# Order bounds, a delayed step, spaced fetches and another DMA queue in a fused DeltaNet / GLA / forgetting-attention layer

## The chip, the cores and the metric

The kernel runs on one core of one Trainium2 chip. The metric is the device time of one execution in microseconds (us). What a measurement of this kernel can tell from no change is about 0.5%, some 5 us.

A core has several engines that run at the same time and wait for each other on semaphores: TensorE (PE in the profile, with its weight loads as PEld), VectorE (DVE), ScalarE (ACT), GpSimd (POOL), and the sync engine (SP), which here only issues DMA transfers. ScalarE and GpSimd can issue DMA transfers too, from the same instruction queue that holds their computations. Each engine works through its own queue in order, so an instruction that waits also holds everything queued behind it on that engine.

## The reference

One layer of a hybrid decoder: RMSNorm, one input projection (2048 to 7585 columns), three token mixers on disjoint groups of heads, a SiLU gate on each, one output projection, the residual, and a final RMSNorm. 16 meta tokens stand in front of 512 tokens. Everything is float32.

```python
h = rms_norm(x, norm_w)                                  # 528 tokens x 2048
(dq, dk, dv, dz, db, da, gq, gk, gv, gz, gl, fq, fk, fv, fz, ff) = split_cols(h @ w_in)
# A) gated DeltaNet, 6 heads x 128, in chunks; state S per head
v_new = u_c - w_c @ s
o     = qd @ s + qk_c @ v_new
s     = s * gl + kd.T @ v_new
o_dn  = gated_head_norm(o, dz, dn_norm_w)                # times silu(dz)
# B) GLA, 5 heads (dk 64, dv 128), decay per key dimension
attn  = einsum('bhid,bhjd,bhijd->bhij', q_c, k_c, exp(g_i - g_j))
o     = (q_c * exp(g)) @ s + attn @ v_c
# C) softmax attention with a forget-gate bias, 5 heads x 128
o_fox = softmax(q @ k.T + c_t - c_s) @ v * silu(fz)
out   = rms_norm(x + concat(o_dn, o_gla, o_fox) @ w_out, final_norm_w)
```

## The kernel before

**Products.** Every float32 weight half (128 x 1024) is loaded by SP into one of two `raw` buffers and split into two parts: `hi` by a cast on ScalarE (`split`, L165, named `whi` or `whio` in the profile) and `lo` by a subtraction on VectorE (L166, `wlo`, `wloo`). The normalised input has two parts too, `xh` and `xl`. A product is then three matmuls: hi by xh, hi by xl, lo by xh (`inproj_part`, L233). A block of 128 columns has 16 slices of the contraction; with meta tokens it has two accumulation chains of 264 columns and so 96 matmuls, without them one chain of 512 columns and 48 matmuls. Each matmul of the input projection is noted in the list `order`; `head` has the place at which a block begins.

**Order.** The instructions of each engine are put in order by a scheduler that plays the program through with its own clock. The kernel steers it in three ways. `later` (L1278) puts a small matmul behind the matmul of a given place in `order` (a lower bound). `sooner` (L1275) puts the matmul of a given place behind the small matmul (an upper bound). `paced` (L171) puts an instruction behind the latest weight split. These bounds only order the queues; they are no semaphores between engines. Blocks come in this order: two `dz` and the `dk`, `dv`, `dq` of the second DeltaNet group, the `gz`, then gk 0, gq 0, gv 0, gv 1, gk 1, gq 1, gv 2, gv 3, gk 2, gv 4, fk 0, fv 0, fq 0, fz 0, fk 1, fq 1, and then the heads of the forgetting attention in pairs of blocks. `gq` and `fq` have one chain, `gk` and `gv` two.

**Mixing.** `dn_mix` (L789) runs the DeltaNet recurrence of a group of three heads over four blocks of 128 tokens: `pks` (L847, keys by state), `zz` on VectorE (L851), `py` (L855), its copy `y` on ScalarE, `psn` (L862), the new state `sn` on VectorE, and, off the recurrence, `po` (L874) and the gate `pt` (L811, L814). For the second group, `soon` (L817) gives `pks`, `py` and `psn` of block b the upper bounds MIX + 56 b + 0, 20 and 38, counted from the first matmul of gv 1; MIX is 10. The triangular inverse before it (`dn_inverse`, L681) has lower bounds of its own: `pm` at PM, `pn` (L753) of the first group at PM + 72.

**GLA.** `gla_pair(p)` (L909) has seven levels per pair of heads (block sizes 64 to 1). For each level VectorE takes two differences (L971, L973), ScalarE an exponential (L974; L977 at the last level), VectorE two products into the shared `kq` buffers (L975, L979), and TensorE many small matmuls `pss` (L993). `PLACE` (L192) gives lower bounds to these groups, and to others, by tile name. Then come the states (`pg0`, `pgn`, `gst`) and the outputs `pgo` (L1057, L1063). The third pair has one head.

**The last step of x.** The later heads of the forgetting attention use products of sums of input blocks. For those, `x_last` (L508) overwrites the second token half of `xh` and `xl` of eight slices: for each slice a load `xe` by GpSimd's queue into a buffer called `row` (seven of these in all), a scaling on ScalarE (L514), L515 on VectorE, a cast (L517) and L518. The first use is the sixth product of the first pair of blocks (`inproj_pair`, L522).

**Tail.** The gated heads' outputs go through DRAM. `fetch` (L1095) loads six of them back during the products of the last pair; `split_o` (L1303) splits them into `oh` and `ol`, all paced. `run` (L1361) is the output projection of these heads, `begin` (L1325) loads a 128 x 512 piece of the residual tokens into `accs` through ScalarE's queue, `add` (L1347) adds a finished bank to it on VectorE. `first_sums` (L591) forms sums of other heads on GpSimd (L596, L597) once their loads `zr` have landed.

Of the kernel before, what the change touches and what calls it, by code (L numbers as in the profile page):

```python
# [82 lines left out]
def tile_hybrid_trunk(ctx, tc, xT, xtok, mtok, w_gate, w_in, w_out, w_dn, consts, lmask, fin_w, out, dbg=None):  # L83
# [104 lines left out]
    def part(name, n=512):  # L188
# [3 lines left out]
    PLACE = {  # L192
        "pss00": (('gv', 3), 50),
        "pss01": (('gv', 3), 56),
        "pss02": (('gv', 3), 72),
        "pss03": (('gv', 3), 82),
        "pss04": (('gv', 3), 92),
        "pss05": (('gk', 2), 6),
        "pss06": (('gk', 2), 16),
        "pg00": (('gk', 2), 44),  # L200
        "pss10": (('fk', 0), 84),
# [7 lines left out]
        "pss23": (('fk', 1), 60),  # L209
        "pss25": (('fk', 1), 84),  # L210
    }
# [296 lines left out]
    def x_last():  # L508

        for k in range(NK):  # L510
            r = row(f"xe{k}")[:, :T]
            nc.gpsimd.dma_start(out=r.rearrange("p (i t) -> p i t", i=2), in_=xT[:, k : k + 9 : 8, HT:])
            x12, x22 = r[:, :HT], r[:, HT:]
            A.activation(x12, x12, AF.Copy, scale=nwc[:, k : k + 1])  # L514
            V.scalar_tensor_tensor(out=x22, in0=x22, scalar=nwc[:, k + 8 : k + 9], in1=x12, op0=ALU.mult,  # L515
                                   op1=ALU.subtract)
            A.copy(xh[k][:, HT:], x22)  # L517
            V.tensor_tensor(out=xl[k][:, HT:], in0=x22, in1=xh[k][:, HT:].bitcast(F32), op=ALU.subtract)  # L518
# [162 lines left out]
    def dn_inverse(g, st):  # L681
# [61 lines left out]
        for q in range(2):  # L743
# [8 lines left out]
            for n in ns:  # L752
                mm = PE.matmul(pn[:, n - q * 6, :], an[64:128, n, 0:64], uf[64:128, n, 64:128],  # L753
                               start=True, stop=True)
                if g + n == 0:
                    behind(mm, PM[g] + 72)
            m2 = t15(f"m2{g}{q}", (64, 6, 64))
# [31 lines left out]
    def dn_mix(g, st):  # L789
# [27 lines left out]
        def soon(mm, b, i):  # L817
            if g == 1:
                sooner.append((mm.ins, MIX + 56 * b + (0, 20, 38)[i]))

# [22 lines left out]
        for b in range(NB):  # L843
# [10 lines left out]
            for j in range(H):  # L854
                mm = PE.matmul(py[:, j * P : (j + 1) * P], uf[:, b * H + j, :], z[:, j, :], start=True, stop=True)  # L855
            soon(mm, b, 1)
            y = t15(f"y{g}{b}")
            A.copy(y, py[:, : H * P].rearrange("p (h d) -> p h d", h=H))
            if b < NB - 1:
                pn = psm.tile([P, 512], F32, tag="m", name=f"psn{g}{b}")  # L860
                for j in range(H):
                    mm = PE.matmul(pn[:, j * P : (j + 1) * P], kd[:, b * H + j, :], y[:, j, :], start=True, stop=True)  # L862
                soon(mm, b, 2)
                sn = t15(f"sn{g}{b}")
# [41 lines left out]

    kts, qts, ats = [], [], []

    def gla_pair(p):  # L909
# [52 lines left out]
        def scores(s, li):  # L962
# [13 lines left out]
            else:  # L976
                A.activation(dv[:, :, 1, :], dv[:, :, 1, :], AF.Exp, scale=SC)  # L977
                kx = kT[:, NM:]
            V.tensor_tensor(out=qxv[:, :, 1, :], in0=qv[:, :, 1, :], in1=dv[:, :, 1, :], op=ALU.mult)  # L979
            return kx, qx  # L980
# [73 lines left out]
        for e in range(ne):  # L1054
            for b in range(NB):
                bs = slice(b * P, (b + 1) * P)
                PE.matmul(po[e][:, bs], at[:, e * NB + b, :], vt[:, e, bs], start=b == 0, stop=False,  # L1057
                          skip_group_check=True)
        for b in range(NB):
# [35 lines left out]
    def fetch(i):  # L1095
        if i < 6:
            if i % 3 == 0:
                zrow.append(six.tile([P, 3, S], F32, tag="six", name=f"zp{i}"))
            nc.sync.dma_start(out=zrow[-1][:, i % 3], in_=zd[SH + i])

# [202 lines left out]
    def split_o(i):  # L1303
# [6 lines left out]
        hi, lo = part(f"oh{i}"), part(f"ol{i}")  # L1310
        paced(A.copy(hi, z), sub(lo, z, hi.bitcast(F32)))
        oparts[i] = hi, lo
# [12 lines left out]
    def begin(tb, cc, load=True):  # L1325
# [4 lines left out]
        if load:  # L1330
            nc.scalar.dma_start(out=acc[tb, cc], in_=xtok[tb * P : (tb + 1) * P, cc * 512 : (cc + 1) * 512])

# [225 lines left out]
```

## Time and profile before

| | |
|---|---|
| three runs | 1014.11, 1014.30, 1019.31 us; median 1014.3 |
| the profiled execution | 1014.57 us, of which the span from first to last instruction is 1012.9 |
| mean granted TensorE clock | 0.992 |
| chain of work that ended last | PE 87%, DMA 4%, DVE 3%, issue 2%, ACT 2% |
| DMA moved | 186.05 MB, mean 184 GB/s |

How to read it. Busy time of an engine is the union of its instructions. A row of waits says who waited for whom: total us, times, longest. A row of the timeline has its start, its length in us, engine, line, operation, tiles (output, arrow, inputs), shapes and, in brackets, how long the engine was idle before it and what ended that. Rows of stretches give from:to, length, busy time of PE, PEld, DVE, ACT and POOL with the number of instructions, then the granted TensorE clock (1.00 is full), the busy share of the DMA engines and GB/s. ACTq and SPq mark an engine's queue as it issues transfers.

### The profile page before, as it was taken

What the parts mean: (1) busy time and instruction counts of PE and PEld (TensorE: products, weight loads), DVE (VectorE), ACT (ScalarE), POOL (GpSimd) and SP (SyncE); (2) the same over time, 40 slices, a digit from 0 to 9 for tenths busy, and PEclk for the clock granted to TensorE, in tenths of its full rate; (3) what the DMA queues carried; (4) which work ended last, traced back from release to release, by engine and by line L of the source; (5) the groups of instructions that cost most, each with busy time, mean ns of one, the idle gap of its engine ahead of it and who ended that gap; (6) DMA issues with size and microseconds to landing.
All of it is one profiled execution on the core that took longest, in us unless ns stands there. A gap on an engine that the chain in (4) does not pass through costs nothing.

```text
span 1012.9 us, 19786 instructions
## 1 busy us (share of the span) xinstructions
PE 987.0 (97%) x7782; PEld 901.0 (89%) x7782; DVE 661.3 (65%) x1427; ACT 478.0 (47%) x1045; POOL 239.3 (24%) x272
## 2 busy tenths in 40 slices
PE   8999999999999999998999999899999999999996
PEld 7899999899999888898999988799999988788885
DVE  6356877966658984334766748576775665868573
ACT  6754534334455334244545444646554452644254
POOL 1032423413324334211213222211223013000060
PEclk9999999999999999999999999999999999999998
DMA  9745557777547798734848685554554557558434
GB/s 352 267 163 203 188 198 239 180 179 158 138 105 175 170 203 228 256 115 146 218 108 192 161 229 144 174 175 148 166 167 142 172 170 278 187 166 270 142 108 166
DMA packets 68513, 186.05 MB, mean 184 GB/s; under 512 B 13725, under 2 KB 16973, under 8 KB 67716
## 3 DMA queue, kind: packets, MB, share of 16 engines
q1 hardware_dynamic: 41920, 121.86, 35.7%
q0 software_dynamic: 15296, 52.63, 22.3%
q10 hardware_dynamic: 11204, 10.30, 3.5%
q8 instruction: 61, 1.00, 0.4%
q14 instruction: 32, 0.26, 0.1%
HBM read 174.07 MB, written 56.69 MB: 228 GB/s over the span
## 4 chain that ended last, share of the span: by engine, by line
PE 87%; DMA 4%; DVE 3%; issue 2%; ACT 2%; SPq 0%; POOL 0%; ACTq 0%; DVEq 0%; POOLq 0%
PE pp L233 43%; PE pp_a L536 7%; PE pq L1335 4%; PE pp L287 4%; PE pt L1335 4%; PE pa L1335 3%; PE ps L1335 2%; PE pp_d L536 2%; PE pp_c L536 2%; PE pp_b L536 2%; PE pr L1335 1%; PE pss L993 1%; DMA xs<-in_xT 1%; DVE wlo L166 1%; PE pfo L1213 1%
## 5 line engine op out<-in xcount | busy, mean ns | idle before, releaser
L233 PE MATMUL pp<-xl,whi 128*128 128x264 f32 (+2 forms) x1120 | 275.2, 307 | 0.0
L233 PE MATMUL pp<-xh,wlo 128*128 128x264 f32 (+2 forms) x1120 | 273.7, 306 | 0.0
L233 PE MATMUL pp<-xh,whi 128*128 128x264 f32 (+2 forms) x1120 | 273.4, 306 | 0.0
L165 ACT CAST whi<-raw 128x1024 fp32r<-128x1024 f32 x131 | 137.3, 1048 | 178.2 <-PE pp L233 107.9
L166 DVE TENSOR_TENSOR wlo<-raw,whi 128x1024 fp32r<-128x1024 f32 x131 | 164.3, 1255 | 59.6 <-ACT whi L165 52.4
L233 PEld LDWEIGHTS pp<-xl,whi 128*128 128x128 f32 x1120 | 183.5, 189 | 9.5 <-issue 0.4
L233 PEld LDWEIGHTS pp<-xh,whi 128*128 128x128 f32 x1120 | 183.1, 189 | 9.2 <-issue 0.2
L233 PEld LDWEIGHTS pp<-xh,wlo 128*128 128x128 f32 x1120 | 182.9, 189 | 9.1 <-DVE wlo L166 0.4
L360 POOL TENSOR_SCALAR stc<-cv 128x528 f32<-128x528 f32 (+1 forms) x18 | 29.1, 1619 | 143.1 <-DVE cv L575 109.9
L1359 POOL TENSOR_TENSOR accs<-accs,fw 128x512 f32<-128x512 f32 x12 | 17.8, 1511 | 111.7 <-ACT sqf L1356 111.7
L575 DVE SCALAR_TENSOR_TENSOR cv<-pb,cpk,cv 128x528 f32<-128x528 f32 (+1 forms) x54 | 41.2, 762 | 0.9
L536 PE MATMUL pp_a<-xh,whi 128*128 128x264 f32 x112 | 29.0, 293 | 1.4 <-ACT whi L165 1.4
L536 PE MATMUL pp_a<-t,whi 128*128 128x264 f32 (+1 forms) x224 | 29.8, 281 | 0.0
L1335 PE MATMUL pa<-whio,oh 128*128 128x512 f32 x72 | 26.7, 405 | 2.6 <-ACT whio L165 2.6
L1335 PE MATMUL pa<-wloo,oh 128*128 128x512 f32 x72 | 29.2, 405 | 0.1
L1335 PE MATMUL pa<-whio,ol 128*128 128x512 f32 x72 | 28.6, 400 | 0.0
L536 PE MATMUL pp_a<-xl,whi 128*128 128x264 f32 x112 | 28.5, 289 | 0.0
L536 PEld LDWEIGHTS pp_a<-t,whi 128*128 128x128 f32 x224 | 28.2, 188 | 0.3
L165 ACT CAST whis<-raws 128x1024 fp32r<-128x1024 f32 x16 | 16.4, 1050 | 22.1 <-PE pq L1335 8.9
L360 POOL TENSOR_SCALAR stdz<-zdz 128x512 f32<-128x512 f32 x6 | 11.2, 1874 | 64.1 <-DVE zdz L378 63.5
L536 PEld LDWEIGHTS pp_a<-xh,whi 128*128 128x128 f32 x112 | 21.4, 191 | 2.0 <-ACT whi L165 1.6
L702 DVE TENSOR_TENSOR ab<-ab 51x30 f32<-51x30 f32 (+14 forms) x60 | 21.3, 354 | 2.6 <-DMA ab<-scmeta 1.2
(486 smaller groups left out, 2110.3 us busy)
## 6 DMA issues: line engine op xcount, KB each, us to landing
raw<-in_w_in SPq DMA_DIRECT2D x103, 512.0 KB, 3.8
ti<-in_w_in POOLq DMA_DIRECT2D x42, 512.0 KB, 5.7
raw<-ti SPq DMA_DIRECT2D x28, 512.0 KB, 3.4
tw<-in_w_dn POOLq DMA_DIRECT2D x24, 512.0 KB, 5.8
ti<-ti POOLq DMA_DIRECT2D x14, 512.0 KB, 7.0
rawo<-in_w_out SPq DMA_DIRECT2D x13, 512.0 KB, 3.6
raws<-tw SPq DMA_DIRECT2D x12, 512.0 KB, 4.3
xt<-in_xtok SPq DMA_DIRECT2D x8, 512.0 KB, 8.5
```

What stands on the lines that cost most here:

```text
L165: pace[0] = A.copy(hi, raw).ins
L166: pace[1] = V.tensor_tensor(out=lo, in0=raw, in1=hi.bitcast(F32), op=ALU.subtract).ins
L233: mm = PE.matmul(p_[:, :nt], wt[:, j * m : (j + 1) * m], xx[k][:, t0 : t0 + nt], start=(k == 0 and wt is hi and xx is xh), stop=(k == KT - ...
L287: mm = PE.matmul(ps[:, :S], wt[:, j * P : (j + 1) * P], xx[k][:, NM:T], start=(k == 0 and wt is hi and xx is xh), stop=(k == KT - 1 and wt ...
L360: G.tensor_scalar_max(t, src, LOW)
L536: m = PE.matmul(p_[:, cols], wt[:, j * P : (j + 1) * P], xx[j][part_][:, cols], start=first and i == 0, stop=i == len(todo) - 1, skip_grou ...
L575: V.scalar_tensor_tensor(out=c, in0=pb[:, t0 + w : w + T], scalar=cwc[:, blk, w : w + 1], in1=c, op0=ALU.mult, op1=ALU.add)
L702: V.tensor_tensor(out=t3, in0=a3[:, j + 1 :, j : j + 1].to_broadcast([NN * 4 + H, m, j]), in1=a3[:, j : j + 1, 0:j].to_broadcast([NN * 4 + ...
L993: mm = PE.matmul(ps[o0 : o0 + n, b * n : b * n + n], kx[rr, k0 : k0 + n], qx[rr, q0 : q0 + n], start=True, stop=True)
L1213: PE.matmul(po[:, qs], v_[:, js], p_[:, jb, qs], start=(jb + i == 0), stop=False)
L1335: PE.matmul(p_, o_[:, s], w_, start=(first and n == 0), stop=(last and n == 2), skip_group_check=True)
L1359: G.tensor_tensor(out=acc[tb, cc], in0=acc[tb, cc], in1=fw[cc], op=ALU.mult)
```

## The change

Five edits, none of which changes an arithmetic instruction.

```diff
@@ PLACE: pair 0 of GLA 16 matmuls later, bounds for the third pair
-        "pss00": (('gv', 3), 50),
-        "pss01": (('gv', 3), 56),
-        "pss02": (('gv', 3), 72),
-        "pss03": (('gv', 3), 82),
-        "pss04": (('gv', 3), 92),
-        "pss05": (('gk', 2), 6),
-        "pss06": (('gk', 2), 16),
-        "pg00": (('gk', 2), 44),
+        "pss00": (('gv', 3), 66),
+        "pss01": (('gv', 3), 72),
+        "pss02": (('gv', 3), 88),
+        "pss03": (('gk', 2), 2),
+        "pss04": (('gk', 2), 12),
+        "pss05": (('gk', 2), 22),
+        "pss06": (('gk', 2), 32),
+        "pg00": (('gk', 2), 60),
...
         "pss23": (('fk', 1), 60),
-        "pss25": (('fk', 1), 84),
+        "pss24": (('fk', 1), 80),
+        "pss25": (('fk', 1), 90),
+        "pgo2": (('pair', 0), 8),
@@ x_last: L515 behind the last product of the last GLA level
-            V.scalar_tensor_tensor(out=x22, in0=x22, scalar=nwc[:, k + 8 : k + 9], in1=x12, op0=ALU.mult,
-                                   op1=ALU.subtract)
+            x = V.scalar_tensor_tensor(out=x22, in0=x22, scalar=nwc[:, k + 8 : k + 9], in1=x12, op0=ALU.mult,
+                                       op1=ALU.subtract)
+            tc.add_manual_dep(x.ins, kqs[-1].name, mybir.DependencyInfo(
+                mybir.DependencyClass.NoSync, mybir.DependencyReason.DATA), reason="behind")
@@ dn_inverse
-                    behind(mm, PM[g] + 72)
+                    behind(mm, PM[g] + 80)
@@ dn_mix: wider upper bounds, and lower bounds for py and psn
-                sooner.append((mm.ins, MIX + 56 * b + (0, 20, 38)[i]))
+                sooner.append((mm.ins, MIX + 62 * b + (0, 22, 42)[i]))
+
+        def late(mm, b, i):
+            if g == 1:
+                later.append((mm.ins, (("gv", 1), MIX + 62 * b + (0, 17, 36)[i])))
...
                 mm = PE.matmul(py[:, j * P : (j + 1) * P], uf[:, b * H + j, :], z[:, j, :], start=True, stop=True)
+                if j == 0:
+                    late(mm, b, 1)
...
                     mm = PE.matmul(pn[:, j * P : (j + 1) * P], kd[:, b * H + j, :], y[:, j, :], start=True, stop=True)
+                    if j == 0:
+                        late(mm, b, 2)
@@ gla_pair, scores: remember L979; bound for pgo
-            V.tensor_tensor(out=qxv[:, :, 1, :], in0=qv[:, :, 1, :], in1=dv[:, :, 1, :], op=ALU.mult)
+            kqs.append(V.tensor_tensor(out=qxv[:, :, 1, :], in0=qv[:, :, 1, :], in1=dv[:, :, 1, :], op=ALU.mult).ins)
...
+                place(f"pgo{p}", mm)
@@ fetch
-            nc.sync.dma_start(out=zrow[-1][:, i % 3], in_=zd[SH + i])
+            paced(nc.sync.dma_start(out=zrow[-1][:, i % 3], in_=zd[SH + i]))
@@ split_o
-        paced(A.copy(hi, z), sub(lo, z, hi.bitcast(F32)))
+        made = A.copy(hi, z), sub(lo, z, hi.bitcast(F32))
+        if i > 1:
+            paced(*made)
@@ begin
-            nc.scalar.dma_start(out=acc[tb, cc], in_=xtok[tb * P : (tb + 1) * P, cc * 512 : (cc + 1) * 512])
+            nc.gpsimd.dma_start(out=acc[tb, cc], in_=xtok[tb * P : (tb + 1) * P, cc * 512 : (cc + 1) * 512])
```

In words: the mixing matmuls `py` and `psn` of the second DeltaNet group stand between a lower and a wider upper bound; the groups of GLA's first pair and the first inverse's `pn` stand behind later products; `x_last`'s L515 stands behind the last L979; the six fetches each follow a weight cast; the first two splits of gated heads are no longer paced; the sixteen loads of residual tokens are issued by GpSimd.

More of the change, by code (lines that the diff above doesn't have):

```diff
@@ L905, in tok_values @@
         A.copy(t16, pw[:NM, :P])
-    kts, qts, ats = [], [], []
+    kts, qts, ats, kqs = [], [], [], []
     def gla_pair(p):
@@ L1056, in gla_pair @@
                 bs = slice(b * P, (b + 1) * P)
-                PE.matmul(po[e][:, bs], at[:, e * NB + b, :], vt[:, e, bs], start=b == 0, stop=False,
-                          skip_group_check=True)
+                mm = PE.matmul(po[e][:, bs], at[:, e * NB + b, :], vt[:, e, bs], start=b == 0, stop=False,
+                               skip_group_check=True)
+                place(f"pgo{p}", mm)
         for b in range(NB):
```

## Prediction

> **What bounds the kernel.** I read the page first, then who waited for whom on TensorE over the whole span, then busy time in short stretches, then the timeline of each stretch.
>
> ```profile
> span 1012.9 us, 19786 instructions
> PE 987.0 (97%) x7782; PEld 901.0 (89%) x7782; DVE 661.3 (65%) x1427; ACT 478.0 (47%) x1045; POOL 239.3 (24%) x272
> ```
> ```profile
> PE py L855 <- DVE zz L851: 3.3, 1, 3.3
> PE pss L993 <- DVE kq L979: 3.1, 3, 2.0
> PE pa L1335 <- ACT whio L165: 2.6, 2, 1.6
> PE pp_a L536 <- ACT whi L165: 1.4, 1, 1.4
> ...
> PE pn L753 <- DVE uf L742: 0.9, 1, 0.9
> PE pgo L1063 <- DVE gst L1050: 0.7, 2, 0.5
> ```
> TensorE is busy 97% of the span. The change neither adds nor removes a matmul, so it can only win or lose idle time, of which the span has 25.9 us; the six rows name 12.0 us of it. A second loss stands in the clock column (after POOL's busy time):
>
> ```profile
> 475.00:478.40 3.40, 1.41 (x11) 1.39 (x12) 3.40 (x10) 1.90 (x8) 0.97 (x2) 1.00 0.48 148
> 478.40:481.80 3.40, 3.40 (x10) 2.65 (x9) 0.99 (x4) 0.41 (x2) 0.15 (x1) 0.51 0.60 201
> 649.00:652.50 3.50, 2.79 (x18) 2.21 (x17) 3.50 (x12) 2.85 (x9) 0.00 (x0) 1.00 0.77 253
> 652.50:655.90 3.40, 3.40 (x18) 3.40 (x17) 0.92 (x1) 1.95 (x9) 1.29 (x3) 0.50 0.81 207
> 823.10:826.60 3.50, 3.34 (x11) 2.77 (x11) 3.47 (x6) 2.58 (x9) 0.00 (x0) 0.51 0.80 277
> ```
> Behind three of the interrupted stretches come 3.4 us at half the granted clock. Here is the first of them:
>
> ```profile
> 473.60 1.04 ACT L165 CAST whi<-raw 128x1024 fp32r<-128x1024 f32 x1
> 474.68 1.22 DVE L166 TENSOR_TENSOR wlo<-raw,whi 128x1024 fp32r<-128x1024 f32 x1 [0.49 <-ACT whi L165]
> ...
> 476.50 0.86 DVE L851 SCALAR_TENSOR_TENSOR zz<-pks,cols,vp 128x128 f32<-128x128 f32 x3
> ...
> 477.00 0.46 PE L855 MATMUL py<-zz,uf 128*128 128x128 f32 x2 [3.31 <-DVE zz L851]
> ...
> 480.30 0.63 PE L233 MATMUL pp<-xh,whi 128*128 128x512 f32 x1
> 480.73 0.63 PE L233 MATMUL pp<-xl,whi 128*128 128x512 f32 x1
> ...
> 482.17 0.39 PE L233 MATMUL pp<-xh,wlo 128*128 128x512 f32 x1
> 482.40 0.39 PE L233 MATMUL pp<-xh,whi 128*128 128x512 f32 x1
> ```
> Two 512-wide matmuls start 0.43 us apart at half clock and 0.23 us apart at full clock. A 3.4 us stretch holds eight at 0.43, so it loses 8 x 0.20 = 1.6 us.
>
> **Mixing between two bounds.** `py` of the last block stands at the old upper bound, matmul 198 counted from gv 1, which is the seventh of gq 1 (gv 1 and gk 1 have 96 each). gq 1 has one accumulation chain, so nothing behind the bound can pass, and `zz` stands on VectorE behind a weight split. The new upper bound is 10 + 62 x 3 + 22 = 218 and the new lower one 213. Sixteen to twenty more matmuls go ahead of `py`, at 0.23 us 3.7 to 4.6 us: more than the 3.3 us stall. Their weights are there: the first 24 matmuls of gq 1 use one half of its weights, the half that the six in front of `py` had used already, and the split at 474.68 is for the other. So the stall goes, and with it the half clock behind it: -3.3 - 1.6 = **-4.9 us**. The ends are 0, if `zz` falls behind the next split, and -4.9. What is late next: the end of mixing moves by up to 20 matmuls of gq 1, 4.7 us, against the products, and GLA pair 0 follows it. Its seven score groups and `pg0` are moved by 16 products too (2.0 us at the 0.122 of the row below), and none of the 3.1 us of `pss` waits lies in pair 0 (2.8 of it is shown below, in pair 2). The cover is the products between them, so I put the shift at nothing; without cover the first group would wait 4.7 - 2.0 = 2.7 us. The bound of `pn` in the first inverse (72 to 80) puts three matmuls of dk 5 and five of dv 3 ahead of its wait of 0.86 us:
>
> ```profile
> 235.78 0.88 PE L753 MATMUL pn<-uf,an 64*64 64x64 f32 x12 [0.86 <-DVE uf L742]
> ...
> 235.94 1.23 DVE L166 TENSOR_TENSOR wlo<-raw,whi 128x1024 fp32r<-128x1024 f32 x1
> ```
> The fifth of dv 3 needs this `wlo`, ready at 237.17. Now `pn` (0.88) and those eight products (1.0) take TensorE from 235.78 to near 237.7; then the fifth and `pn` come after 237.17 and end near 238.1. Ends -0.9 and +0.4; I take 0.
>
> **x behind GLA's last operand.**
>
> ```profile
> 628.66 0.89 DVE L515 SCALAR_TENSOR_TENSOR xe<-xe,cpk 128x264 f32<-128x264 f32 x2
> ...
> 630.34 0.42 DVE L971 TENSOR_TENSOR gvt<-gqk 64x256 f32<-64x256 f32 x1
> ...
> 635.05 0.51 ACT L514 ACTIVATE xe<-xe,cpk 128x264 f32<-128x264 f32 x1 [6.63 <-DMA xe<-in_xT]
> 635.47 0.41 ACT L977 ACTIVATE gvt<-gvt 64x256 f32<-64x256 f32 x1
> ...
> 636.20 0.41 DVE L979 TENSOR_TENSOR kq<-gqk,gvt 64x256 f32<-64x256 f32 x1
> ```
> ```profile
> 630.57 0.45 PE L993 MATMUL pss<-kq,kq 64*32 64x32 f32 x32 [0.77 <-DVE kq L979]
> 636.76 0.46 PE L993 MATMUL pss<-kq,gqk 64*32 64x32 f32 x32 [2.02 <-DVE kq L979]
> 651.06 0.48 PE L1063 MATMUL pgo<-gst,gqk 64*128 64x128 f32 x2 [0.52 <-DVE gst L1050]
> ```
> ```profile
> 689.98 2.93 PE pp_a L536 x24
> ```
> The 0.77 us wait is there because two L515 (0.89 us) ran ahead of that level's operands; the new dependence removes them. The 2.02 us wait has another cause: L971 ended at 630.8, but its exponential L977 sat on ScalarE behind an L514 that waited 6.63 us for its transfer. The dependence is on L515 and not on L514. If ScalarE's order changes with it, both waits go (-2.8), `pgo` behind the ninth product of the pair (up to 9 x 0.122 = 1.1 us later) covers its 0.7, and the half clock after 652.5 goes: together **-5.1**. If ScalarE's order stays, L977 still ends at 635.9 and the last group starts about 0.3 earlier; the four L515 (0.45 us each) then run only after it, the rows of `xe` come free late for the later transfers, and `pgo` keeps a wait: 0. The trace cannot tell which, since the order comes from the scheduler's own clock. I take half, **-2.5**. The bounds of the two groups before (80 and 90 of fk 1) cost nothing: products of fk 1 run in front of them, six more at most, 0.7 us.
>
> **Fetches, casts, residual.** The fetches stay six, each one SP issue; they now follow one weight cast each, and raw loads queue between them. Two `oh`/`ol` splits lose their pace. The waits that they can touch are 1.4 (`pp_a`), 1.6 (the first `pa`) and the half clock after 823.1, 1.6: end -4.6. The other end is one such wait more, +1.4. The weights still pass through the same two raw buffers, so I take 0. The residual:
>
> ```profile
> 841.92 0.83 ACTq L1331 DMA_DIRECT2D accs<-in_xtok  x2
> ...
> 856.26 4.74 ACTq L1331 DMA_DIRECT2D accs<-in_xtok  x6
> 861.10 1.04 ACT L165 CAST whio<-rawo 128x1024 fp32r<-128x1024 f32 x1 [5.10 <-DMA accs<-in_xtok]
> ```
> ```profile
> L512 POOL DMA_DIRECT2D xe<-in_xT x8 | 6.0, 746 | 13.8 <-DVE xl L518 6.6 <-DVE kq L975 3.9 <-DMA zd<-zfz 3.4
> ```
> ```profile
> POOL zr L596 <- DMA zr<-zd: 16.0, 2, 15.7
> ...
> PE pa L1335 <- ACT whio L165: 1.0, 1, 1.0
> ```
> Sixteen issues leave ScalarE's queue. There they waited for free tiles and held the weight cast for 5.10 us, and TensorE 1.0 us: **-1.0**, ends 0 and -1.0. They go to GpSimd, where an issue of the nearest kind, `xe`, takes 0.75 us: 12 us for the sixteen, which fit in the 15.7 us that GpSimd stood waiting for `zr` in the same stretch, and in the idle time around it; behind them stand the first sums, which no product of this stretch uses. The Trainium skill, DMA: Bandwidth & Descriptors, section Issuing engines are not separate DMA queues, says that another issuing engine saves only the sequencer's issue time, usually small; by it this edit gives nothing and the sum is 1.0 higher. The row speaks against it: what ScalarE lost was an in-order wait, not issue time.
>
> **Sum.** -4.9 + 0 - 2.5 + 0 - 1.0 = -8.4 us, from the profiled execution's 1014.57 us (span 1012.9 and 1.7 around it): 1006.2. That execution is 0.3 us over the median of 1014.3, so I predict **1006 us**.
>
> **Rivals.** *The stall moves.* `zz` falls behind the next weight split (2.3 us for cast and split), now earlier since TensorE runs on; `py` waits again, in the single chain, and the half clock stays. For it: that is the order on VectorE now. Against: 16 more matmuls of cover. Time 1006.2 + 4.9 = 1011.
>
> *GpSimd's queue holds the residual (slower).* If the loads stand behind L596 there, the first is issued when L596 runs, near 853.6 instead of 841.9:
>
> ```profile
> 846.28 0.69 DVE L1349 TENSOR_TENSOR accs<-accs,pa 128x512 f32<-128x512 f32 x1 [0.72 <-DMA accs<-in_xtok]
> ...
> 853.55 0.74 POOL L596 TENSOR_TENSOR zr<-zr 128x256 f32<-128x256 f32 x1 [15.68 <-DMA zr<-zd]
> ```
> The add already waited 0.72 us for its load, and it frees the bank for the next `pa`, so I count each us of lateness beyond the first as one of TensorE: 10.7, plus half clock twice (3.2), without the gain of 1.0: 1006.2 + 14.9 = 1021. It is slower than before once the first load comes over 6 us late. Against it: the loads can go as soon as tiles are free, long before `zr` lands.
>
> *All waits go*: B at -5.1, both casts and `pn` covered: 1006.2 - 2.6 - 4.6 - 0.9 = 998.
>
> *Half clock is not tied to these stalls.* In the rows it follows 2.0 us of idling in 3.4 us, but also 0.7 us in 3.5, so the tie is not proven. Without it the terms lose 1.6 and 0.8: 1008.6. The Trainium skill, TensorE: Matmul & The Clock Gate, section What's actually happening, puts half rate after at least one idle window of about 3.4 us; no idle here is that long, so by that rule these stalls throttle nothing, but the row of 478.4 has 0.51.
>
> **Numbers.** Forecast 0.56, its own range 1002 to 1011; the stall moves 0.18; GpSimd's queue 0.11; all waits go 0.10; no tie to the clock 0.05. What can be told from no change is 0.5%, 5.1 us: faster ends at 1009.2, slower begins at 1019.4. Faster: 0.52 of the forecast, 0.10, and 0.03 of the last: 0.65. Within: 0.04 + 0.18 + 0.02 = 0.24. Slower 0.11. The range for 8 in 10 is 998 to 1013.5: it leaves out the slow case and the edges of two others.
>
> **What would show it.** Right: no wait of `py` on `zz` over 1 us, clock 1.00 behind it, no `pss` wait of 2 us, ScalarE free of `accs`. Wrong: a new wait over 2 us on `pss` in pair 0, L977 still behind an L514 that waits for its transfer, or `accs` issued on GpSimd after L596. A new wait of several us in a stretch that no edit names would make the prediction wrong altogether, since the whole order is drawn up anew.

## The result and the profile after

The changed kernel ran at a median of 1007.4 us (1005.1 to 1013.1, six runs) against 1016.0 us (1014.1 to 1019.3, six runs) for the kernel before on the same chip: a ratio of 0.9915, 95% interval 0.9886 to 0.9944, so 8.6 us faster. Predicted were 1006 us, 8.4 us less. The sum is right; three of its terms are not. Two of the twelve runs of one kernel below, e9, were slow (2464 and 1198 us) and are left out of its figures.

The profiled execution is the slowest of the six, 1013.11 us. In the page of the changed kernel, the span, the busy times and the chain that ended last by engine:

```profile
span 1011.4 us, 19801 instructions
PE 986.9 (98%) x7782; PEld 899.8 (89%) x7782; DVE 662.7 (66%) x1427; ACT 479.9 (47%) x1045; POOL 249.6 (25%) x288
...
PE 76%; DMA 9%; DVE 8%; ACT 3%; issue 2%; POOL 1%; ACTq 0%; SPq 0%; DVEq 0%; POOLq 0%
```

TensorE's work is the same as before (986.9 against 987.0 us). In the chain TensorE fell from 87% to 76%, while DMA rose from 4 to 9% and VectorE from 3 to 8%: the chain now leaves TensorE in more places. TensorE's waits, by whom it waited for (total us, times, longest):

```profile
PE pfx L1210 <- DVE fmt L1205: 1.9, 4, 0.9
PE pss L1005 <- DVE kq L991: 1.9, 3, 0.9
PE pp L235 <- DVE wlo L166: 1.8, 3, 0.7
PE pp L235 <- ACT whi L165: 1.8, 2, 1.3
PE pss L1005 <- issue: 1.7, 3, 1.1
...
PE pa L1350 <- ACT whio L165: 1.0, 1, 1.0
```

The 3.3 us of `py` on `zz` and the 2.0 us of `pss` on `kq` are gone, and `pa` on `whio` went from 2.6 to 1.0. New are small `pss` waits and waits for the weights of gq 0 near 405 us. Waits of 0.3 to 1.5 us there show in the profiles of most of the kernels below too, e3 and e12 without mixing among them, so they are not put down to one edit. In this execution they account for much of the time, as the stretches there show (columns as before: the number behind POOL's busy time is the clock):

```profile
404.20:407.60 3.40, 1.54 (x9) 0.91 (x8) 2.17 (x3) 3.21 (x5) 0.58 (x1) 0.99 0.24 93
407.60:411.00 3.40, 3.40 (x53) 2.50 (x53) 1.73 (x6) 0.59 (x2) 2.50 (x5) 0.50 1.13 386
411.00:414.40 3.40, 3.40 (x10) 2.63 (x9) 1.64 (x3) 0.87 (x2) 0.00 (x0) 0.50 0.90 361
```

6.8 us at half clock follow, 3.2 us by the prediction's own count of 1.6 each. In a second profiled execution of the same kernel (below) the same wait is 0.5 us long and no half clock follows. So single executions scatter by some us, and what an edit does has to be read from its own stage.

**Stages.** The matmuls are the same in all kernels, so the time from one product to another can be compared, as long as the same matmuls lie between the two. Four products cut the span: one in the middle of gk 1 (it starts at 461.6 us in the kernel before), the 25th of fq 0 (596.3), one in the first pair of blocks (658.7), one in the last pair (817.1); the end of the last matmul of all ends it. In all kernels the same number of matmuls stands ahead of each cut, with one exception: in e5, e10 and e11 16, 2 and 16 small matmuls of the third pair's outputs have moved behind the cut at 658.7, 1 to 2 us for sixteen. (The first product of fq 0 would not do as a cut: in e5 and e11 48 small matmuls have moved behind it.) Each number is the difference of two such times in one profiled execution, in us. Between the first two lie the end of mixing and the first two pairs of GLA; then the third pair and the last step of x; then the forgetting attention; then the tail. The last column is where half clock stood.

| kernel | to gk 1 | gk 1 to fq 0 | to first pair | to last pair | tail | half clock from (us) |
|---|---|---|---|---|---|---|
| before | 461.6 | 134.7 | 62.4 | 158.4 | 187.5 | 478.4, 652.5, 823.2 |
| after | 468.6 | 134.2 | 57.3 | 158.8 | 184.2 | 11.6, 407.6 (6.8 long) |
| e1, the same again | 463.0 | 134.4 | 60.3 | 159.3 | 184.2 | 642.8 |
| e2, mixing | 466.7 | 133.1 | 63.0 | 158.7 | 188.2 | 406.0 (6.8), 641.5, 866.8 |
| e6, mixing's bounds | 460.7 | 130.9 | 62.7 | 158.2 | 189.1 | 647.6, 859.2 |
| e3, x | 462.5 | 134.4 | 57.3 | 158.2 | 189.5 | 479.3, 858.2 |
| e4, tail | 460.7 | 133.5 | 63.9 | 158.0 | 184.2 | 651.9 |
| e9, residual | 462.8 | 135.4 | 61.1 | 158.1 | 190.4 | 11.2, 478.8, 639.3, 823.6 |
| e12, x and tail | 462.8 | 134.2 | 57.9 | 158.8 | 184.5 | none |
| e8, no dependence | 463.4 | 132.1 | 65.0 | 158.6 | 183.4 | 635.3 (6.8) |
| e7, pn as before | 463.8 | 132.1 | 57.5 | 158.2 | 183.5 | none |
| e5, pair 1 16 later | 461.4 | 132.0 | 53.9 | 167.8 | 183.5 | 683.4 (6.8) |
| e10, e7 and pair 1 8 later | 460.9 | 132.8 | 61.0 | 164.7 | 184.1 | 636.2, 687.4 (6.8) |
| e11, e7 and pair 1 16 later | 462.8 | 133.6 | 53.9 | 167.6 | 183.8 | 572.8, 688.8 |

The row "after" against "before": -0.5 where mixing was to bring 4.9, -5.1 where x was to bring 2.5, -3.3 where the tail was to bring 1.0, and +0.4 in the stage between these two. These give -8.5 together; its first column lost 7.0: 1.1 by the first product of this line (64.7 instead of 63.6 us), the rest mostly to the waits near 405 us and the half clock behind them. (All executions fall to half clock again in the last microseconds, when TensorE has ended.)

### The profile page after: what moved, and what is told of

Same layout as the page of the kernel before. It is cut to its first block, busy times and chain, and to the rows that moved or that the text cites. A ratio compares the mean times of both kernels' runs of the same rounds, so it can differ in the third digit from the quotient of the medians.

```text
span 1011.4 us, 19801 instructions
## 1 busy us (share of the span) xinstructions
PE 986.9 (98%) x7782; PEld 899.8 (89%) x7782; DVE 662.7 (66%) x1427; ACT 479.9 (47%) x1045; POOL 249.6 (25%) x288
## 4 chain that ended last, share of the span: by engine, by line
PE 76%; DMA 9%; DVE 8%; ACT 3%; issue 2%; POOL 1%; ACTq 0%; SPq 0%; DVEq 0%; POOLq 0%
PE pp L235 33%; PE pp_a L540 7%; PE pq L1350 4%; PE pp L289 4%; PE pa L1350 4%; PE pt L1350 4%; PE ps L1350 2%; DVE wlo L166 2%; PE pp_d L540 2%; PE pp_c L540 2%; PE pp_b L540 2%; DMA sc<-ab 1%; DMA xm<-sc 1%; DMA xb<-in_xT 1%; PE pr L1350 1%
## 5 line engine op out<-in xcount | busy, mean ns | idle before, releaser
L362 POOL TENSOR_SCALAR stdz<-zdz 128x512 f32<-128x512 f32 x6 | 8.9, 1497 | 66.8 <-DVE zdz L380 66.3
L847 POOL TENSOR_TENSOR eg<-eg,qT 128x384 f32<-128x384 f32 x8 | 8.4, 1044 | 57.9 <-DVE egl L846 45.2
```

The source lines that it names most:

```text
L362: G.tensor_scalar_max(t, src, LOW)
L847: G.tensor_tensor(out=eg, in0=eg, in1=qT[:, :, ts], op=ALU.mult)
```

## The experiments

Three sets of kernels, each set on one chip with its own runs of the kernel before, five rounds each. The theory: the three parts act in their own stages and add. The rivals are in the expectations.

### The change again, and its three parts

e1 is the changed kernel itself. e2 is the kernel before with the mixing part alone (pair 0 of `PLACE`, `pn`, both bounds):

```diff
-        "pss00": (('gv', 3), 50),
+        "pss00": (('gv', 3), 66),
...
-                    behind(mm, PM[g] + 72)
+                    behind(mm, PM[g] + 80)
...
-                sooner.append((mm.ins, MIX + 56 * b + (0, 20, 38)[i]))
+                sooner.append((mm.ins, MIX + 62 * b + (0, 22, 42)[i]))
...
+                later.append((mm.ins, (("gv", 1), MIX + 62 * b + (0, 17, 36)[i])))
```

e3 is the kernel before with the x part alone (the dependence of L515, the bounds of the third pair):

```diff
-        "pss25": (('fk', 1), 84),
+        "pss24": (('fk', 1), 80),
+        "pss25": (('fk', 1), 90),
+        "pgo2": (('pair', 0), 8),
...
+            tc.add_manual_dep(x.ins, kqs[-1].name, mybir.DependencyInfo(
+                mybir.DependencyClass.NoSync, mybir.DependencyReason.DATA), reason="behind")
```

e4 is the kernel before with the tail part alone (fetches, splits, residual):

```diff
-            nc.sync.dma_start(out=zrow[-1][:, i % 3], in_=zd[SH + i])
+            paced(nc.sync.dma_start(out=zrow[-1][:, i % 3], in_=zd[SH + i]))
...
+        if i > 1:
+            paced(*made)
...
-            nc.scalar.dma_start(out=acc[tb, cc], in_=xtok[tb * P : (tb + 1) * P, cc * 512 : (cc + 1) * 512])
+            nc.gpsimd.dma_start(out=acc[tb, cc], in_=xtok[tb * P : (tb + 1) * P, cc * 512 : (cc + 1) * 512])
```

> The changed kernel as it is, measured again beside the kernel before. Theory 1 (three gains add up: mixing 4.9 us, the step of x 2.5 to 5.1, the tail 1.0): 8 to 11 us under the kernel before. Theory 2 (the profiled execution of the change at 1013.1 us holds two half-clock stretches, at 11 and 407 us, that belong to that execution): they are missing in another profile, and its time is 1005 to 1008 us. If the half clock at 407 us comes from the change, it is there again and the time stays above 1010.

> The kernel before with the mixing edits alone: both bounds, pair 0 of GLA 16 products later, pn of the inverse 8 later. Theory 1: the 3.3 us wait of py and the half clock behind it go, -4.9 us. Rival: GLA's pair 1, whose places were not moved, now waits for its operands and gives 2 to 4 us of it back: -1 to -3 us, with new waits of pss on DVE between 565 and 590 us.

> The kernel before with the edits on the last step of x and GLA's pair 2 alone (L515 behind the last L979, bounds for pss24, pss25, pgo2). If ScalarE's order follows (the last exponential ahead of the third L514), the waits 0.8 + 2.0 + 0.7 and the half clock go: -5.1 us. If not: 0 to -0.4 us.

> The kernel before with the tail's edits alone (fetches each behind a weight cast, first two splits unpaced, residual loads on GpSimd's queue). Theory 1: only the residual counts, -1.0 us (TensorE's wait for whio near 861). Rival: the loads on ScalarE's queue and the burst of fetches also held the first whio, so the wait of 1.6 shrinks and the half clock near 823 goes: -3 us. Against both: GpSimd issues late and the add waits: slower by several us.

Against 1015.2 us for the kernel before (33 runs; here and below the ratio is a measurement of its own and not the quotient of the two medians):

| kernel | median us | ratio | 95% interval |
|---|---|---|---|
| e1, whole change | 1009.8 | 0.9931 | 0.9906 to 0.9955 |
| e2, mixing | 1013.0 | 0.9992 | 0.9967 to 1.0016 |
| e3, x | 1011.9 | 0.9961 | 0.9941 to 0.9980 |
| e4, tail | 1011.1 | 0.9958 | 0.9935 to 0.9980 |

The ratios are worth -0.8 (mixing), -4.0 (x) and -4.3 us (tail), in sum -9.1 against -7.0 for the whole; with some 2 us of uncertainty on each, adding is not refuted. What is refuted is mixing's term of -4.9: its interval ends at -3.3 us. Yet the local edit did exactly what was forecast. In the timeline of the changed kernel `py` of the last block now stands deeper in gq 1 and starts without a wait:

```profile
485.03 0.39 PE L235 MATMUL pp<-xl,whi 128*128 128x512 f32 x1
485.26 0.38 PE L863 MATMUL py<-zz,uf 128*128 128x128 f32 x2
```

From the product at 461.6 to the first of gv 3, at 505.7, with as many matmuls in between, the kernel before took 44.1 us, and the changed kernel, e1 and e2 took 38.7, 38.7 and 39.4: 5.3 us are gained. At the 25th product of fq 0 only 0.5, 0.3 and 1.6 us of them are left. Some go in pair 0 of GLA (below), most in pair 1, the place that the rival in e2's expectation names. The chain that ended last there, by start and length, in the changed kernel:

```profile
553.47 8.30 DMA xb<-in_xT
561.83 0.38 issue
562.21 0.45 DVE a L972
...
564.05 0.61 DVE gvt L953
564.67 1.14 DVE wlo L166
565.80 0.34 DVE t L507
566.15 1.18 DVE gqk L954
...
569.80 0.34 DVE kq L991
```

In the kernel before the chain in the same stage stays on TensorE:

```profile
551.08 0.79 PE psd L958 x8
551.87 14.16 PE pp L233 x116
```

VectorE's timeline in the kernel before, then in the changed kernel, points to the cause. L503 (L505 after) is a step of the earlier sums of x blocks (`x_sums`); L942 (L954) is the running sum of pair 1's decay, from which all of its groups follow:

```profile
554.78 0.50 DVE L503 SCALAR_TENSOR_TENSOR xb<-xb,cpk,xa 128x264 f32<-128x264 f32 x1
...
557.91 1.27 DVE L942 TENSOR_TENSOR_SCAN gqk<-gsc,gvt 128x528 f32<-128x528 bf16 x1
```

```profile
561.80 0.49 DVE L505 SCALAR_TENSOR_TENSOR xb<-xb,cpk,xa 128x264 f32<-128x264 f32 x1 [4.56 <-DMA xb<-in_xT]
...
566.06 1.25 DVE L954 TENSOR_TENSOR_SCAN gqk<-gsc,gvt 128x528 f32<-128x528 bf16 x1
```

TensorE arrives earlier, but VectorE stands idle for 4.56 us before L505, waiting for a transfer, with the scan queued behind it. Counted from the product in gk 1 (461.6 us before, 468.6 after), this step of x starts 93.2 us later in both kernels: TensorE is ahead, VectorE is not. The DMA issues of that moment (KB, us to landing) show how much slower the transfer is, before and after:

```profile
xb<-in_xT POOLq DMA_DIRECT2D x1, 264.0 KB, 3.0
```

```profile
xb<-in_xT POOLq DMA_DIRECT2D x1, 264.0 KB, 8.3
```

The stretches in which it was on its way, before and after (second to last column: busy share of the DMA engines; it is over 1 where packets that start in a stretch end behind it):

```profile
550.20:553.20 3.00, 3.00 (x27) 3.00 (x27) 2.50 (x6) 1.87 (x4) 2.93 (x4) 1.00 0.69 182
```

```profile
553.40:557.40 4.00, 4.00 (x30) 3.37 (x28) 3.62 (x10) 1.97 (x6) 2.44 (x3) 1.00 1.05 226
557.40:561.80 4.40, 4.40 (x39) 4.40 (x38) 0.00 (x1) 0.52 (x1) 0.00 (x0) 1.00 1.11 270
```

The DMA engines were 0.69 busy before and fully busy after, and VectorE did nothing in the last 4.4 us. In e1, e6 and e7 the load took 8.0, 8.4 and 7.3 us, in e12, which lacks mixing, 3.1. By these rows the groups of pair 1, whose places were not moved, wait for a VectorE that waits for this load.

### Where mixing's gain goes

e5 is the changed kernel with pair 1's eight bounds 16 products later:

```diff
-        "pss10": (('fk', 0), 84),
+        "pss10": (('fv', 0), 4),
...
-        "pss16": (('fv', 0), 48),
-        "pg01": (('fv', 0), 76),
+        "pss16": (('fv', 0), 64),
+        "pg01": (('fv', 0), 92),
```

e6 is the kernel before with mixing's two bounds alone, the `sooner` and `later` lines of e2, and pair 0 and `pn` where they were. e7 is the changed kernel with `pn` back, e8 the changed kernel without the dependence of x:

```diff
-                    behind(mm, PM[g] + 80)
+                    behind(mm, PM[g] + 72)
```

```diff
-            tc.add_manual_dep(x.ins, kqs[-1].name, mybir.DependencyInfo(
-                mybir.DependencyClass.NoSync, mybir.DependencyReason.DATA), reason="behind")
```

> The changed kernel, with the eight bounds of GLA's second pair (pss10 to pss16, pg01) also 16 products later. Theory 1 (mixing's gain of about 5 us is handed back in the second pair, because its groups stayed where they were while the vector work behind mixing moved later): the new waits of pss on kq between 559 and 584 us (together 3 to 4 us) shrink to under 1 us, the stretch of products from the end of mixing to the end of the second pair loses 3 us or more less than in the changed kernel, and the time is 2 to 4 us under that of the changed kernel. Theory 2 (VectorE's order sets those waits, whatever the products in front of the groups): the waits move 16 products on with the groups and stay above 2.5 us; the time stays within 1 us. Rival: the groups of the second pair now run into what follows (the outputs of the pair, fq 0's single chain), with a new wait of 2 us or more there, and the time is 1 to 3 us longer.

> The kernel before with mixing's two bounds alone: GLA's first pair and the first inverse stay where they were. Theory 1: py's wait of 3.3 us is gone, as in the kernel with the whole mixing part; without the shift of the first pair there is a new wait of pss there, by the prediction's count up to 2.7 us, and the second pair, which need not follow a later first pair, waits less than with the shift (under 2 us in sum, against 3.5). Time within 2 us of the kernel with the whole mixing part. Rival: the shift of the first pair is what drives the second pair late; without it both pairs wait under 1 us and the time is 3 to 5 us under the kernel before.

> The changed kernel with pn of the first inverse back at its old bound (72 instead of 80). Theory 1: one wait of pn on uf of 0.8 to 0.9 us in place of the two waits on wlo of together 1.0 to 1.1 us, so 0.2 us less, nothing that the time can show; the rest as in the changed kernel, its time within 2.5 us. Rival: the later pn also moves the later waits near 403 to 407 us (gq 0 on its weight parts, 0.5 to 1.5 us, none in the kernel before), since all vector work behind the inverse comes later; with the old bound they are gone and the time is 2 to 4 us lower.

> The changed kernel without the dependence of x_last's L515 on the last product of GLA's last level; the bounds pss24, pss25 and pgo2 stay. Theory 1 (the dependence is what moved the last exponential ahead of the scaling that waits for its transfer): the exponential stands again behind an L516 that waits for its load, the last pss of the third pair waits about 2 us again, and the time is 3 to 5 us over the changed kernel. Rival (the bounds alone did it, or the scheduler's own clock): the exponential stays ahead, no wait of pss above 1 us, and the time is within 2.5 us of the changed kernel.

Against 1015.0 us (29 runs):

| kernel | median us | ratio | 95% interval |
|---|---|---|---|
| e5, pair 1 16 later | 1012.1 | 0.9951 | 0.9926 to 0.9976 |
| e6, mixing's bounds alone | 1013.1 | 0.9973 | 0.9942 to 1.0005 |
| e7, pn as before | 1005.0 | 0.9883 | 0.9847 to 0.9919 |
| e8, no dependence | 1014.2 | 0.9981 | 0.9956 to 1.0006 |

The stage from gk 1 to fq 0 in three parts, cut at the first product of gv 3 and the first of fk 0, with as many matmuls in each part in all kernels; then, from the same profiled executions, how long the load `xb` took to land, and when the scan started after the first product of fk 0, all in us:

| kernel | mixing | pair 0 | pair 1 | load | scan |
|---|---|---|---|---|---|
| without mixing: before, e3, e4, e9, e12 | 42.8 to 44.1 | 49.9 to 50.0 | 40.4 to 41.4 | 3.0 to 3.1 | 2.3 to 2.6 |
| e6, bounds alone | 38.7 | 49.3 | 42.9 | 8.4 | 6.4 |
| e2, mixing | 39.4 | 50.8 | 42.9 | 7.7 | 6.7 |
| after | 38.7 | 51.4 | 44.1 | 8.3 | 7.3 |
| e1, the same again | 38.7 | 50.9 | 44.8 | 8.0 | 7.5 |
| e8, no dependence | 38.7 | 51.6 | 41.7 | 6.7 | 5.3 |
| e7, pn as before | 38.7 | 50.7 | 42.7 | 7.3 | 5.9 |
| e5, pair 1 16 later | 38.7 | 51.9 | 41.3 | 6.2 | 4.7 |
| e10, e7 and pair 1 8 later | 38.7 | 51.7 | 42.4 | 7.1 | 6.0 |
| e11, e7 and pair 1 16 later | 38.7 | 51.1 | 43.7 | 7.4 | 6.7 |

In the main, the later the scan, the longer the part of pair 1 takes, whether the places of pair 1 were moved (the last three rows) or not. And the part of pair 0 takes 50.7 to 51.9 us in the eight executions in which its groups were moved, 49.3 to 50.0 in the six in which they were not, e6 with mixing's bounds among these: the shift costs some 1 to 2 us itself.

**e5**: as the theory expected, the `pss` waits of pair 1 fall, to 0.35 and 0.81 us, and the stage to 132.0 us, 2.3 under the changed kernel. But the load of x landed sooner too, in 6.2 us. e7, with pair 1 where it was, takes 132.1 us, and e11, with the places of e5, 133.6. So e5 does not show that later places help. And the next thing is late, as the rival has it: the transposes `pfx` of the first forgetting head. The stretches of e5 there:

```profile
680.00:683.40 3.40, 1.22 (x11) 1.04 (x10) 2.00 (x5) 1.67 (x3) 0.00 (x0) 1.00 0.35 136
683.40:686.80 3.40, 2.72 (x9) 1.76 (x8) 2.00 (x8) 1.26 (x3) 0.00 (x0) 0.50 0.46 146
686.80:690.20 3.40, 3.40 (x18) 3.40 (x17) 0.93 (x4) 0.43 (x3) 0.00 (x0) 0.50 0.02 5
```

A wait of 2.18 us on `fmt`, then 6.8 us at half clock: the stage to the last pair takes 167.8 instead of 158.8 us, 1 to 2 of which are the sixteen matmuls that moved into it. The expectation had named other places for such a wait.

**e6**: pair 1 waits without the pair 0 shift too, 2.5 us (1.19, 0.74 and 0.54), more than expected. The stage takes 130.9 us, 2.2 less than e2's, of which 1.5 lie in pair 0, and pair 0 waits only 0.18 us, not the bound of 2.7. Its ratio of 0.9973 and e2's of 0.9992 have overlapping intervals, so the time decides nothing here; what is said here rests on the stage, in one execution of each.

**e7** has the lowest ratio of the study, 11.9 us under the kernel before, and its six runs lie within 3.4 us. Its interval overlaps those of the changed kernel (0.9886 to 0.9944 and, as e1, 0.9906 to 0.9955), beside which it was not run; that it is faster than that kernel is not shown. Locally it does what was expected: one wait of `pn` of 0.86 us in place of 0.43 and 0.68 us for the weight parts. That is 0.25 us. The rival is not it either: the waits near 404 us are still there (0.56 and 0.53). Whether the rest belongs to the bound was tried in e11.

**e8** is decided. Without the dependence the last exponential (L987 there) stands behind a scaling of x that waits for its transfer, in e8's ScalarE timeline:

```profile
635.40 0.51 ACT L516 ACTIVATE xe<-xe,cpk 128x264 f32<-128x264 f32 x1 [7.39 <-DMA xe<-in_xT]
635.82 0.42 ACT L987 ACTIVATE gvt<-gvt 64x256 f32<-64x256 f32 x1
```

In the changed kernel it runs ahead (L989), and the scaling waits alone:

```profile
636.74 0.44 ACT L989 ACTIVATE gvt<-gvt 64x256 f32<-64x256 f32 x1 [1.62 <-DVE gvt L983]
640.94 0.52 ACT L516 ACTIVATE xe<-xe,cpk 128x264 f32<-128x264 f32 x1 [3.76 <-DMA xe<-in_xT]
```

In e8 the last `pss` waits 5.5 us, with half clock behind it; the stage takes 65.0 instead of 57.3 us. The dependence on L515 does move ScalarE's order.

### The residual alone, the parts without mixing, and two later places

e9 is the kernel before with the last edit of e4 and nothing else (`accs` issued by `nc.gpsimd`). e12 is the kernel before with all edits of e3 and e4. e11 is e7 with the bounds of e5, e10 the same with half of that shift:

```diff
-        "pss10": (('fk', 0), 84),
+        "pss10": (('fk', 0), 92),
...
-        "pg01": (('fv', 0), 76),
+        "pg01": (('fv', 0), 84),
```

> The kernel before with the sixteen residual loads on GpSimd's queue and nothing else. Theory 1 (the prediction's term of 1.0 is right, and the other 3 us of the whole tail part come from the paced fetches and the two splits that lost their pace): the loads of the weights near 861 us wait no longer behind accs, TensorE waits 0.4 instead of 1.0 us there, the first wait of pa on whio near 823 us is still about 1.6 us with half clock behind it, and the time is about 1 us under the kernel before. Theory 2 (the residual is worth the whole 4 us: with ScalarE's queue free of the sixteen issues every output weight is cast earlier): the time is 3 to 5 us under the kernel before, with the stretch from 836 us to the end 3 us shorter, and the wait near 823 us as before.

> The kernel before with the x part and the tail part of the change, without its mixing part (bounds, GLA's first pair, pn). Theory 1 (mixing's net gain in the whole change is near nothing, as its pn bound costs what its other bounds bring): about 8 us under the kernel before, within 2 us of the changed kernel, and about 3 us over the changed kernel with pn at its old bound. Theory 2 (the three parts do not add; each alone takes the same half clock stretches away or the same weight waits): less than 6 us under the kernel before. Rival: mixing takes back more than it brings: at the time of the changed kernel with the old pn bound, 1005, or under it.

> The changed kernel with pn back at 72 and GLA's second pair 8 products later. Theory 1 (the second pair's groups need a later place, and the gain survives when they move only half as far): the pss waits between 559 and 584 us fall from about 2.5 to about 1 us, no new wait above 1 us near 680 us, and the time is 1 to 2 us under the changed kernel with pn at 72 (which ran at 1005.0 with 1015.0 for the kernel before). Theory 2 (what follows takes it back, as with 16): a new wait of 1 to 2 us at the first pfx of the forgetting attention, 0 to 3 us longer.

> The changed kernel with pn back at 72 and GLA's second pair 16 products later. Theory 1 (pn at 80 is worth 3 to 5 us of loss in any setting): 3 to 5 us under the changed kernel with the second pair 16 later (1012.1 with 1015.0 for the kernel before). Theory 2 (what pn's bound changes is only how the scheduler draws up the order of all that follows, so its effect does not carry to another setting): no difference beyond 2.5 us to that kernel. Either way the wait of 2.2 us at pfx near 681 us, if it comes from the second pair being late, shows again; if it is gone, it came from the order of casts on ScalarE there.

Against 1016.5 us (29 runs; ten of e9):

| kernel | median us | ratio | 95% interval |
|---|---|---|---|
| e9, residual alone | 1018.0 | 0.9998 | 0.9973 to 1.0022 |
| e12, x and tail | 1008.5 | 0.9923 | 0.9899 to 0.9947 |
| e10, e7 and pair 1 8 later | 1013.1 | 0.9974 | 0.9956 to 0.9991 |
| e11, e7 and pair 1 16 later | 1012.3 | 0.9965 | 0.9946 to 0.9984 |

**e9**: no gain that the time can show. ScalarE's queue is free of `accs`, and the same cast now waits for its weights; its row in e9:

```profile
863.95 1.04 ACT L165 CAST whio<-rawo 128x1024 fp32r<-128x1024 f32 x1 [3.64 <-DMA rawo<-in_w_out]
```

`pa` waited 1.6 us for it, more than the 1.0 before; its wait near 823 us is 2.2 instead of 1.6, with half clock behind it as before. The interval (-2.7 to +2.2 us) leaves room for the 1 us of theory 1; these waits speak against it, and theory 2's 3 to 5 us lie outside. So the tail's 4.3 us come from the paced fetches and the two unpaced splits, or from these together with the residual; fetches and splits alone were not tried. What they do is seen in ScalarE's timeline. Before, two `oh` casts run between the last weight cast of the pair and the first of the output weights:

```profile
819.28 1.05 ACT L165 CAST whi<-raw 128x1024 fp32r<-128x1024 f32 x1 [2.24 <-PE pp_a L536]
820.24 1.14 ACT L1311 CAST oh<-zp 128x512 fp32r<-128x512 f32 x2
821.28 1.04 ACT L165 CAST whio<-rawo 128x1024 fp32r<-128x1024 f32 x1
```

After, they have gone ahead of it, into a gap:

```profile
818.56 1.13 ACT L1324 CAST oh<-zp 128x512 fp32r<-128x512 f32 x2
819.84 1.06 ACT L165 CAST whi<-raw 128x1024 fp32r<-128x1024 f32 x1 [0.16 <-DMA raw<-in_w_in]
822.52 1.05 ACT L165 CAST whio<-rawo 128x1024 fp32r<-128x1024 f32 x1 [1.61 <-PE pp_a L540]
```

e4 has this second order, e9 the first. `pa`'s first wait fell from 1.6 to 1.0 us, with no half clock behind it, and the second output weight was cast 8.4 us after the product that begins the tail instead of 14.8. Every kernel with the tail part spends 183.4 to 184.5 us in the tail; those without it, 187.5 to 190.4.

**e12**: -7.8 us without mixing (interval -10.3 to -5.4). The whole change had -8.6 and -7.0 in its two sets. Mixing's net part in it is therefore about zero, within the 2 to 3 us that these intervals leave.

**e10, e11**: e11 ran at 0.9965, e5 with the other `pn` bound at 0.9951: no loss of 3 to 5 us from `pn` at 80, as theory 2 expected, and what e7 may have over the changed kernel does not carry to another setting. The `pfx` wait of 2.2 us came back in both. e10 came out 9 us over e7 by the ratios, longer than either of its theories had: besides the `pfx` wait, with 6.8 us at half clock behind it, the third pair's last groups waited 0.97 and 1.81 us, and the stage of x lost most of its gain (61.0). Moving pair 1 by 8 was no better than by 16.

## Why the prediction was right, and which steps of it were not

**The sum** was right because its errors cancel. Against the change's own stages: -4.9 became -0.5, -2.5 became -5.1, -1.0 and the fetches' 0 became -3.3, and the stage for which there was no term gave +0.4.

**Mixing (-4.9): the step that failed** is "so I put the shift at nothing". Locally the term holds: no wait of `py`, clock 1.00 behind it, 5.3 us gained by gv 3. What was late next was sought in pair 0, where it was put at nothing with the groups moved and at 2.7 us without cover. In e6, where they were not moved, pair 0 waits 0.2 us; the move itself, meant as cover, costs some 1 to 2 us, with waits of up to 1.1 us that have no releaser but "issue". Pair 1, 50 us on, was not looked at, though its places stand fixed in the same table and it shares VectorE with the load of x. Its part takes 41.3 to 44.8 us in the nine executions with mixing's bounds against 40.4 to 41.4 in the five without, and in the main the longer the later the scan behind L505 starts. So the place of the give-back is measured; that the load is its cause is read from VectorE's rows and from this order, and the load itself was not moved. That the collision on the DMA engines is what slowed the load is read from the busy shares and was not tried by itself either. The first rival, that the stall moves, had this price (4.9) but the wrong place.

**pn (0, ends -0.9 and +0.4)** was in its bounds: +0.25 us in the waits.

**x (-2.5)** was half of two branches, and the branch with ScalarE's order changed is the true one: no `pss` wait above 0.24 us there, half clock gone, -5.1 us in the stage after and -5.0 in e3. e1 shows the scatter: one wait of 1.7 us for `gkm` and half clock left it -2.1. Taking half between branches is a mean, not a forecast. e8, with the bounds and without the dependence, shows that the bounds alone do not change ScalarE's order; the dependence without the bounds was not tried.

**Fetches and splits (0, ends -4.6 and +1.4)**: "The weights still pass through the same two raw buffers, so I take 0" was the wrong reason. The buffers were the same, but ScalarE's queue ahead of the first output weight was shorter by two casts. About -3.3 us fell within the range given.

**Residual (-1.0)**: alone it is 0.2 us by the ratio, with an interval of -2.7 to +2.2 that does not exclude the term, but its wait came back, longer, as one for the weights. "What ScalarE lost was an in-order wait" was right, but the weight behind that wait was not there earlier. The Trainium skill, DMA: Bandwidth & Descriptors, section Issuing engines are not separate DMA queues, has another issuing engine save only issue time; e9's ratio of 0.9998 agrees with it. The rival of a held queue did not come: GpSimd issued the first `accs` at 834.7 us, before its first sum at 850.4.

**All waits go** (998) and **half clock is not tied** (1008.6) are both short of the case: `pp_a` still waits 1.1 us, and the tie is real but depends on the phase, as the last section shows. Where `py` stalled, half clock cost 1.3 us and not 1.6.

## What to carry to other kernels

When a stall is removed, follow the engine that gains to the next place where its order is fixed, and list what the other engines and the loads do by then: here of 5 us won at 480 us 1 to 2 were lost to the groups that were moved along, and most of the rest near 565 us, behind one 264 KB load with a scan queued after it. Measure an edit between two instructions that all versions share, since whole times scatter by 3 us and errors of several terms cancel in them; and see that the same work lies between the two, since an edit of the order can move work across the cut. Of the kernels measured, the change with `pn` left where it was has the lowest ratio (0.9883, interval 0.9847 to 0.9919); that it beats the change as it is is not shown, and e11 against e5 shows no such effect of that bound.

## What the runs showed of the hardware

Half clock comes in windows of 3.413 us on a grid that runs through an execution: all starts of half clock in one execution lie whole multiples of it apart, and the grid lies differently in each execution. Most of it is told by the idle time of TensorE inside one window. The same 3.3 us stall of `py` shows it. In the kernel before, one window held 1.97 us of idle and was followed by half clock (the stretch at 475.00 in the prediction). In e12 the stall fell across an edge of the grid (the two stretches are such windows), 1.83 and 1.49 us in the two, and the clock stayed full:

```profile
473.30:476.70 3.40, 1.58 (x14) 1.37 (x12) 1.53 (x8) 3.07 (x12) 1.49 (x2) 1.00 0.39 125
476.70:480.10 3.40, 1.90 (x13) 1.80 (x14) 3.33 (x11) 1.75 (x6) 1.11 (x2) 1.00 0.61 191
480.10:483.50 3.40, 3.40 (x17) 2.74 (x16) 1.27 (x3) 0.78 (x3) 0.26 (x1) 1.00 0.51 159
```

Over the 14 profiled executions, from 16 us on, every window with 1.86 us of idle or more was followed by half clock; between 1.6 and 1.85 us some were; below that, seven were: three with 0.71 us at the outputs `pgo` of GLA's third pair (before, e4 and e6), and four that were at half clock themselves (0 to 0.68 us of idle). The two kinds below 1.6 us stay unexplained. The Trainium skill, TensorE: Matmul & The Clock Gate, section What's actually happening, has the free-running window of 3413 ns, and the runs agree; it has half rate come after an idle window, and here a window that was a little over half idle was enough. So what a stall costs is a matter of phase: from the product at 461.6 to gv 3 the kernel before, e3 and e9, with half clock behind the stall of 3.3 us, took 44.1 us, and e4, with the same stall and without half clock, 42.8.
